# Token-ordered projection of the values, one-step transposes and another bank for statistics, in a one-core encoder layer

## The chip, the cores and the metric

The kernel runs on one core of a Trainium2 chip. The metric is the device time of one execution in microseconds (us). Below, TensorE is PE, VectorE is DVE, ScalarE is ACT, GpSimd is POOL and SyncE is SP in the profile; PEld is TensorE's loading of stationary operands.

## The reference

One layer of an encoder on x with 512 tokens of 2048 features, all float32. A normalised x is projected once, and two mixers read the projection:

```python
xn = rms_norm(x, attn_norm_g[l])
proj = jnp.einsum("bsd,dc->bsc", xn, w_in[l])            # 2048 -> 5 x 1024
u_val, u_gate, q, k, v = jnp.split(proj, split_pts, axis=-1)
y_conv = conformer_conv(u_val, u_gate, ...)   # gate, conv of 31 taps, LayerNorm over channels, silu
y_na = neighborhood_attention(heads(q), heads(k), heads(v), rpb[l])
mixed = concat([rms_norm(y_conv, ...), rms_norm(y_na, ...)])
x = x + mixed @ w_out[l]
# then: norm, up-projection to 2 x 5632, conv of 3 taps, silu(gate) * val, down-projection, residual, norm
```

The attention has 16 heads of 64. The tokens form a grid of 8 rows by 64 columns; a query at column c sees all 8 rows of 16 columns around c (clamped at the edges), with a learned bias by relative position.

## The kernel before, in words

**Data.** x lies with features on partitions: 16 tiles of 128 features x 512 tokens. The products are made to float32 accuracy out of three matmuls in a rounded format (mm3, L122): each operand is split into a high part and the rest, and high x high, high x low and low x high are summed in PSUM. Activations are split once (split, L155). Weights come in units of 128 x 1024 (512 KB, a DMA on SP, L109); ScalarE copies the high part (L114), VectorE subtracts for the low part (L115). weights() (L146) makes a unit three units (AHEAD) before it is used. A unit serves 8 slices of 128 features, so 24 matmuls of 128x512.

**Order of work.** The program is written as one stream of projection units. After each unit (or piece of one) tick (L132) advances two lists of generators, steps and asteps, by one yield each: what a generator does up to its next yield is put behind that unit's last matmul. A scheduler then lays out each engine's queue by priorities and these bounds; "pinned" instructions stay together, and shifted(600) lowers the priority of the convolution's taps. Each engine executes its queue in the order given.

**The input projection** follows ORDER (L51), "aaqaqaqaaqaqaqqq". An a is a pair of 128 gate channels and 128 value channels (glu, L321: two times 16 slices x 3 matmuls); gated (L326) multiplies by rstd, the reciprocal root of the tokens' mean square, takes the sigmoid, and runs the 31 taps on VectorE (L340, L343). A q is q, k and v of a pair of heads (qkv, L387), each 48 matmuls into one of three PSUM banks "mm"; VectorE evicts them, multiplied by rstd: q with tokens regrouped into four blocks of 16 columns (L395), k plainly (L399), v as four windows of 32 columns (L404).

**Attention of a pair** (attend, L409) is a generator: four loads of bias tables; eight transposes of v (L423) into two banks "tr", evicted by ScalarE as vt (L425); a yield; eight score matmuls (L437; each is two passes, so the profile counts 16) into a tile "sc" of two banks and the two "tr" banks, and the softmax of four 128x512 pieces: scale and bias (L444), maximum (L446) on VectorE, exp with sums on ScalarE (L449), reciprocal on VectorE (L450), normalisation on ScalarE (L452). After two or three yields turn(2) (L455) transposes the last two pieces (eight transposes, L462, evicted at L467 as pt); a yield later turn(0) the first two; two yields later the values (L476: 16 matmuls of 64 columns by 128, counted 32, into a bank "po") and their eviction ao (L496) with its sum of squares.

**Statistics.** rsqrt_steps (L170) sums over partitions with matmuls against ones (L182) into the bank tile "sc", computes the reciprocal root, and, after a yield, spreads it over partitions by two more matmuls (L201 to L217). group_a (L349) is the LayerNorm of the convolution's output: it sums the eight tiles on VectorE (L353, L355), takes the mean by a matmul (L358) into "sc", and goes on to ma, the split normalised tiles, and ra, the group's RMS factor. It is appended after pair NORM_AT = 5.

**Behind it:** norm_b (L534) normalises the attention's output into mb, yielding after every second tile. out_half (L523) projects ma, then mb, 16 tiles of 24 matmuls each, into the "mm" banks; read_a (L542) adds the first half to the residual as oa, from when ra is there. Then the gated MLP runs in chunks of four hidden tiles: up products (L672, L677), conv and activation, in_two (L773) splitting the hidden tile for the down products pd of the chunk, which follow in the next chunk. In the loop of chunks (L794) in_two of the first three tiles stands ahead of the fourth tile's up products, that of the fourth behind them.

PSUM has eight banks: "mm" three, "sc" a tile of two, "tr" two, "po" one. 512-token tiles in SBUF share one pool of 79.

Of the kernel before, what the change touches and what calls it, by code (L numbers as in the profile page):

```python
# [10 lines left out]
F32 = mybir.dt.float32  # L11
# [39 lines left out]
ORDER = "aaqaqaqaaqaqaqqq"  # L51
NORM_AT = 5
# [13 lines left out]
def layer(ctx: ExitStack, tc: tile.TileContext, xT, w_in, w_out, w_up, w_down, par, tab, out):  # L66
# [103 lines left out]
    def rsqrt_steps(accs, n, name, to=slice(0, S), keep=True):  # L170
# [22 lines left out]

        if not keep:
# [9 lines left out]
        yh = sm.tile([P, S // P], F32R, tag="rsh", name="rsh")  # L204
        nc.vector.tensor_copy(yh, y)
        nc.vector.tensor_sub(y, y, yh.bitcast(F32))
        ds = []
        for part in (yh.bitcast(F32), y):
# [4 lines left out]
        ps = psa.tile([P, 2, S], F32, tag="sc", name="st")[:, 0]  # L213
# [46 lines left out]
    for k in range(KD):  # L260
        x1.append(t2("x"))
        last = pin(nc.sync.dma_start(x1[k], xT[k]))
# [8 lines left out]
    a_, q_ = iter(range(NC_)), iter(range(NP_))  # L271
    for step in ORDER:
        i = next(a_ if step == "a" else q_)
        for n in ((NC_ + i, i) if step == "a" else (2 * NC_ + j * NP_ + i for j in range(3))):
            for u in range(KD // U):
                plan.append(lambda n=n, u=u: unit(w_in[n, :, u * U * P:(u + 1) * U * P], U * P))
# [4 lines left out]
    rstd, late = [], []  # L281

    def stats1():
# [6 lines left out]
        rstd.append((yield from rsqrt_steps(acc1, D, "rstd1")))  # L290
# [3 lines left out]
    def project(n):  # L294
# [9 lines left out]
        return ps  # L304

# [20 lines left out]
    def gated(i, pg, pv):  # L326
# [5 lines left out]
        nc.vector.tensor_mul(h, pv, g)  # L332
# [16 lines left out]
    def group_a():  # L349
# [7 lines left out]
        ps = psa.tile([P, 2, S], F32, tag="sc", name="st")[:, 0]  # L357
# [26 lines left out]
    def grid(t, c0, w):  # L384
        return t.rearrange("p (r c) -> p r c", c=GW)[:, :, c0:c0 + w]

    def qkv(p):  # L387
        got = []
        for j, nm in enumerate("qkv"):
            ps = project(2 * NC_ + j * NP_ + p)  # L390
            if nm == "q":

                t = t2(nm)
                by = "p (r b c) -> p r b c"
                nc.vector.tensor_mul(t.rearrange("p (b r c) -> p r b c", b=NB, r=WH),  # L395
                                     ps.rearrange(by, b=NB, r=WH), rstd[0].rearrange(by, b=NB, r=WH))
            elif nm == "k":
                t = t2(nm)
                nc.vector.tensor_mul(t, ps, rstd[0])  # L399
            else:  # L400

                t = [t2("vw").rearrange("p (b k) -> p b k", b=2) for _ in range(NB // 2)]
                for b in range(NB):
                    nc.vector.tensor_mul(t[b // 2][:, b % 2].rearrange("p (r c) -> p r c", c=KW), grid(ps, KC0[b], KW),  # L404
                                         grid(rstd[0], KC0[b], KW))
            got.append(t)
        return got

    def attend(p, q, k, v):  # L409


        hps = [slice(j * DH, (j + 1) * DH) for j in range(2)]
        tabs = {}
        for n in (2, 3, 0, 1):
            tabs[n] = t2("tab").rearrange("p (i k) -> p i k", i=2)
            i = nc.sync.dma_start(tabs[n], tab[2 * p + n % 2][:, n // 2:n // 2 + 2])
            if p == 0:
                pin(i)
        vt = []
        for half in range(2):  # L420
            ps = psa.tile([P, 4, P], F32, tag="tr", name="trv", bufs=2)
            for c in range(4):
                nc.tensor.transpose(ps[:, c, :], v[half][:, c // 2, c % 2 * P:(c % 2 + 1) * P], ident)  # L423
            t = t2("vt").rearrange("p (c k) -> p c k", c=4)
            nc.scalar.activation(t, ps, AF.Copy)  # L425
            vt.append(t)
        po = psa.tile([P, S], F32, tag="po", name="po")

        def scores():

            wide = psa.tile([P, 2, 2, 2 * P], F32, tag="sc", name="sc")
            banks = [wide[:, j] for j in range(2)]
            banks += [psa.tile([P, 2, 2 * P], F32, tag="tr", name="sc", bufs=2) for _ in range(2)]
            first = True
            for b in range(NB):
                for j, hp in enumerate(hps):
                    m = nc.tensor.matmul(banks[b // 2 * 2 + j][:, b % 2, :], q[hp, b * P:(b + 1) * P],  # L437
                                         grid(k, KC0[b], KW)[hp], start=True, stop=True)
# [508 lines left out]
```

## Time and profile before

| | |
|---|---|
| time, median of three runs | 2054.8 us (2051.95 to 2055.14) |
| the profiled execution | 2052.8 us, its span 2051.0 us |
| clock granted to TensorE | 0.998 of full speed |
| matmuls | 10816 |
| DMA traffic | 275.38 MB |

The profile is of one execution. Its page gives busy time by engine, forty slices of the span, DMA queues, the chain of work that ended last, and groups of instructions by line. Groups are read as line, engine, operation, output<-inputs, shapes, count | busy us, mean ns of one | idle time of the engine before them and who ended it. A row of the timeline gives the start and the length in us, the engine, the line, the operation and how many follow each other (x8); in brackets the idle time ahead of it and its releaser. Matmuls overlap, and their ends are modelled, so costs on TensorE are read from start to start.

### The profile page before, as it was taken

What the parts mean: (1) busy time and instruction counts of PE and PEld (TensorE: products, weight loads), DVE (VectorE), ACT (ScalarE), POOL (GpSimd) and SP (SyncE); (2) the same over time, 40 slices, a digit from 0 to 9 for tenths busy, and PEclk for the clock granted to TensorE, in tenths of its full rate; (3) what the DMA queues carried; (4) which work ended last, traced back from release to release, by engine and by line L of the source; (5) the groups of instructions that cost most, each with busy time, mean ns of one, the idle gap of its engine ahead of it and who ended that gap; (6) DMA issues with size and microseconds to landing.
All of it is one profiled execution on the core that took longest, in us unless ns stands there. A gap on an engine that the chain in (4) does not pass through costs nothing.

```text
span 2051.0 us, 28588 instructions
## 1 busy us (share of the span) xinstructions
PE 2031.7 (99%) x10816; PEld 1736.7 (85%) x10816; DVE 1666.7 (81%) x2319; ACT 1060.8 (52%) x1726; POOL 156.2 (8%) x186
## 2 busy tenths in 40 slices
PE   9999999999999999999999999999999999999997
PEld 7888888888788998888888888888888888888887
DVE  7996697686577898888878878888888888889876
ACT  6244424457436555555555555555554555555562
POOL 0000000000001001111111111111111111110110
PEclk9999999999999999999999999999999999999999
DMA  7332333236237435555555565565565565555682
GB/s 253 113 103 83 99 98 111 84 103 237 82 118 184 119 116 130 135 149 136 129 147 141 128 145 143 129 143 144 124 144 144 124 150 141 136 129 134 147 212 83
DMA packets 97209, 275.38 MB, mean 134 GB/s; under 512 B 10928, under 2 KB 11696, under 8 KB 97072
## 3 DMA queue, kind: packets, MB, share of 16 engines
q1 hardware_dynamic: 71712, 227.40, 35.0%
q0 software_dynamic: 25216, 46.15, 14.8%
q8 instruction: 85, 1.39, 0.3%
q14 instruction: 52, 0.43, 0.1%
q10 hardware_dynamic: 144, 0.01, 0.0%
HBM read 218.99 MB, written 54.53 MB: 133 GB/s over the span
## 4 chain that ended last, share of the span: by engine, by line
PE 97%; DVE 1%; DMA 0%; issue 0%; ACT 0%; DVEq 0%; ACTq 0%
PE pu L672 25%; PE pu L677 13%; PE pd L127 8%; PE pd L125 8%; PE pd L126 8%; PE pj L125 7%; PE pj L127 7%; PE pj L126 7%; PE po L125 3%; PE po L127 3%; PE po L126 3%; PE pu L125 1%; PE pu L127 1%; PE pu L126 1%; PE sc L437 1%; PE po L476 1%
## 5 line engine op out<-in xcount | busy, mean ns | idle before, releaser
L114 ACT ACTIVATE whi<-raw 128x1024 fp32r<-128x1024 f32 x364 | 384.4, 1058 | 486.8 <-PE pj L126 178.5
L115 DVE TENSOR_TENSOR wlo<-raw,whi 128x1024 fp32r<-128x1024 f32 x364 | 444.3, 1222 | 221.4 <-ACT whi L114 198.8
L672 PE MATMUL pu<-xc,whi 128*128 128x512 f32 x2240 | 574.7, 392 | 0.0
L672 PEld LDWEIGHTS pu<-xc,whi 128*128 128x128 f32 x2240 | 409.1, 189 | 74.0 <-ACT pl L684 0.2
L677 PEld LDWEIGHTS pu<-xc,wlo 128*128 128x128 f32 x2240 | 305.6, 190 | 21.9
L677 PE MATMUL pu<-xc,wlo 128*128 128x256 f32 x2240 | 312.3, 282 | 0.0
L125 PE MATMUL pd<-hh,whi 128*128 128x512 f32 x640 | 249.0, 391 | 2.6 <-ACT hh L775 2.6
L125 PE MATMUL pj<-xh,whi 128*128 128x512 f32 x640 | 251.1, 396 | 0.0
L127 PE MATMUL pj<-xh,wlo 128*128 128x512 f32 x640 | 249.7, 390 | 0.0
L126 PE MATMUL pj<-xl,whi 128*128 128x512 f32 x640 | 249.7, 390 | 0.0
L126 PE MATMUL pd<-hl,whi 128*128 128x512 f32 x640 | 249.2, 389 | 0.0
L127 PE MATMUL pd<-hh,wlo 128*128 128x512 f32 x640 | 249.2, 391 | 0.0
L791 POOL DMA_DIRECT2D x2d<-pdc x160 | 139.3, 872 | 1167.7 <-ACT pdc L790 949.5
L684 ACT ACTIVATE pl<-pu 128x256 f32<-128x256 f32 x280 | 104.5, 382 | 166.0 <-PE pu L672 165.9
L114 ACT ACTIVATE whi<-ws 128x1024 fp32r<-128x1024 f32 x132 | 139.8, 1059 | 78.1 <-PE pu L672 57.9
L343 DVE SCALAR_TENSOR_TENSOR y<-ch,prm,y 128x504 f32<-128x504 f32 (+14 forms) x240 | 173.7, 742 | 4.6
L115 DVE TENSOR_TENSOR wlo<-ws,whi 128x1024 fp32r<-128x1024 f32 x132 | 161.0, 1220 | 19.8 <-ACT whi L114 19.7
L127 PEld LDWEIGHTS pd<-hh,wlo 128*128 128x128 f32 x640 | 120.1, 188 | 28.8 <-DVE wlo L115 3.0
L125 PEld LDWEIGHTS pj<-xh,whi 128*128 128x128 f32 x640 | 120.2, 188 | 27.9 <-issue 3.7
L127 PEld LDWEIGHTS pj<-xh,wlo 128*128 128x128 f32 x640 | 120.2, 188 | 25.9 <-DVE wlo L242 0.4
L126 PEld LDWEIGHTS pj<-xl,whi 128*128 128x128 f32 x640 | 120.4, 188 | 25.0 <-DVE xl L265 0.7
L125 PEld LDWEIGHTS pd<-hh,whi 128*128 128x128 f32 x640 | 120.5, 188 | 24.9 <-ACT hh L775 3.0
(182 smaller groups left out, 2742.9 us busy)
## 6 DMA issues: line engine op xcount, KB each, us to landing
raw<-in_w_up SPq DMA_DIRECT2D x176, 512.0 KB, 3.6
raw<-in_w_down SPq DMA_DIRECT2D x88, 512.0 KB, 3.7
x2d<-pdc POOLq DMA_DIRECT2D x160, 256.0 KB, 4.7
raw<-in_w_in SPq DMA_DIRECT2D x76, 512.0 KB, 3.7
raw<-in_w_out SPq DMA_DIRECT2D x32, 512.0 KB, 3.9
x<-in_xT SPq DMA_DIRECT2D x32, 256.0 KB, 5.3
tab<-in_tab SPq DMA_DIRECT2D x32, 256.0 KB, 5.2
x2d<-x SPq DMA_DIRECT2D x16, 256.0 KB, 2.1
```

The lines of the kernel that those rows point to most:

```text
L114: i = nc.scalar.activation(hi[:, :n], raw[:, :n], AF.Copy)
L115: j = nc.vector.tensor_sub(lo[:, :n], raw[:, :n], hi[:, :n].bitcast(F32))
L125: nc.tensor.matmul(ps, hi[:, a], mh, start=start, stop=False)
L126: nc.tensor.matmul(ps, hi[:, a], ml, start=False, stop=False)
L127: return nc.tensor.matmul(ps, lo[:, a], mh, start=False, stop=stop)
L343: nc.vector.scalar_tensor_tensor(y[:, a:b], h[:, a + j - PAD:b + j - PAD], prm[:, o + j:o + j + 1], y[:, a:b], op0=ALU.mult, op1=ALU.add)
L437: m = nc.tensor.matmul(banks[b // 2 * 2 + j][:, b % 2, :], q[hp, b * P:(b + 1) * P], grid(k, KC0[b], KW)[hp], start=True, stop=True)
L476: m = nc.tensor.matmul(grid(po, b * BLK, BLK)[hp], vt[b // 2][:, 2 * (b % 2) + ch, hp], pts[b // 2 * 2 + j][:, 2 * (b % 2) + ch, :], start ...
L672: return nc.tensor.matmul(ps, w[0][:, k * P:(k + 1) * P], comb[c][k], start=k == 0, stop=k == U - 1)
L677: nc.tensor.matmul(ps[:, H:], w[1][:, k * P:(k + 1) * P], comb[c][k][:, :H], start=False, stop=False)
L684: nc.scalar.activation(to, ps, AF.Copy)
L791: nc.gpsimd.dma_start(xd[d], t, accum_op=ALU.add)
```

## The change

- **Order.** The values are no longer projected with each pair. ORDER becomes "aavaavaqaqaqaqqqqq": each v is a project_v of half of all value channels, after two gate/value pairs. The weights of the values come in units for two slices of features x 512 channels; x is now the stationary operand (128 tokens at a time) and the weights move, so that the result has tokens on partitions. Four banks are summed at once: the three "mm" and "po" for the first half, the two "tr" and "sc" for the second. ScalarE evicts them in ten pieces, scaled by the token's rstd: four tiles vg, and three tiles vx in which token groups are shifted by half a tile, for the windows of the middle blocks.
- **Token order.** For the projection tokens are ordered by groups of 8 columns (xG). The convolution's input, the attention's output and the tables are permuted where they are written or read; q is evicted plainly and k with a permutation. The transposes of v, vw and vt go.
- **Attention** becomes one generator over all pairs: tables; a yield; the values of the pair before directly ahead of this pair's scores, and the softmax in place in its tables, whose normalisation is one VectorE product with the reciprocal broadcast; three yields; all 16 transposes of the pair in one step, half of them into "sc"; a yield. The last pair's values come at the end.
- **Statistics** use the bank "po" instead of "sc" (with two sums, "po" then "sc"); the low part of the reciprocal root has a tile of its own. group_a is appended after pair 4.
- **norm_b** yields once, after the fifth tile. **In the first chunk** of the MLP in_two of all four tiles stands behind the fourth tile's up products.

The diff, cut to its core:

```diff
-ORDER = "aaqaqaqaaqaqaqqq"
-NORM_AT = 5
+ORDER = "aavaav" + "aq" * 4 + "qqqq"
+NORM_AT = 4
+NG = GW // 8
...
-        banks = [psa.tile([P, 2, S], F32, tag="sc", name="st")[:, 0]]
+        banks = [psa.tile([P, S], F32, tag="po", name="st")]
         if len(accs) > 1:
-            banks.append(psa.tile([P, S], F32, tag="po", name="st"))
+            banks.append(psa.tile([P, 2, S], F32, tag="sc", name="st")[:, 0])
...
+    vg, vx = [], []
+
+    def project_v(half):
+
+        if half:
+            sc = psa.tile([P, 2, S], F32, tag="sc", name="pv")
+            banks = [psa.tile([P, S], F32, tag="tr", name="pv", bufs=2) for _ in range(2)] + [sc[:, 0], sc[:, 1]]
+        else:
+            banks = [psm.tile([P, S], F32, tag="mm", name="pv") for _ in range(3)]
+            banks.append(psa.tile([P, S], F32, tag="po", name="pv"))
+        for u in range(KD // 2):
+            wh, wl = weights()[:2]
+            for k in range(2):
+                kk, f = 2 * u + k, slice(k * S, (k + 1) * S)
+                for t, ps in enumerate(banks):
+                    xh, xl = (x[:, t * P:(t + 1) * P] for x in xs[kk])
+                    nc.tensor.matmul(ps, xh, wh[:, f], start=kk == 0, stop=False)
+                    nc.tensor.matmul(ps, xl, wh[:, f], start=False, stop=False)
+                    m = nc.tensor.matmul(ps, xh, wl[:, f], start=False, stop=kk == KD - 1)
+            tick(m)
+            while late and rstd:
+                late.pop(0)()
+        y = rtok[0]
+        vg.append([t2("vg") for _ in banks])
+        vx.append([t2("vx") for _ in banks[1:]])
+        for t, ps in enumerate(banks):
+            nc.scalar.activation(vg[half][t], ps, AF.Copy, scale=y[:, t:t + 1])
+            for x, rows in ((t - 1, slice(0, DH)), (t, slice(DH, P))):
+                if 0 <= x < len(vx[half]):
+                    nc.scalar.activation(vx[half][x][rows], ps[rows], AF.Copy, scale=y[rows, t:t + 1])
...
-        nc.vector.tensor_mul(h, pv, g)
+        by = "p (g r c) -> p r g c"
+        nc.vector.tensor_mul(h.rearrange("p (r g c) -> p r g c", r=WH, g=NG), pv.rearrange(by, r=WH, g=NG),
+                             g.rearrange(by, r=WH, g=NG))
...
+    def values_of(p, b):
+        g, x = vg[p // 4], vx[p // 4]
+        return {0: (g[0], g[1]), 1: (x[0], x[1]), 2: (x[1], x[2]), 3: (g[2], g[3])}[b]
...
+    def softmax(banks, ts):
+        for n in (2, 3, 0, 1):
+            s = ts[n]
+            nc.vector.scalar_tensor_tensor(s, banks[n], DH ** -0.5, s, op0=ALU.mult, op1=ALU.add)
+            nm = sm.tile([P, 2], F32, tag="nm", name="nm")
+            nc.vector.tensor_reduce(nm, s, axis=AX.X, op=ALU.max, negate=True)
+            su = sm.tile([P, 2], F32, tag="su", name="su")
+            for i in range(2):
+                nc.scalar.activation(s[:, i], s[:, i], AF.Exp, bias=nm[:, i:i + 1], accum_out=su[:, i:i + 1])
+            nc.vector.reciprocal(su, su)
+            nc.vector.tensor_mul(s, s, su.unsqueeze(2).broadcast_to([P, 2, 2 * P]))
+
+    def turn(ts):
+        pts, first = {}, True
+        for n in (2, 3, 0, 1):
+            if n == 0:
+                wide = psa.tile([P, 2, 4, P], F32, tag="sc", name="trp")
+            ps = wide[:, n] if n < 2 else psa.tile([P, 4, P], F32, tag="tr", name="trp", bufs=2)
+            for i in range(2):
+                for ch in range(2):
+                    m = nc.tensor.transpose(ps[:, 2 * i + ch, :], ts[n][:, i, ch * P:(ch + 1) * P], ident)
                     if not first:
                         pin(m)
                     first = False
-            for n in (2, 3, 0, 1):
-                s = t2("s").rearrange("p (i k) -> p i k", i=2)
-                nc.vector.scalar_tensor_tensor(s, banks[n], DH ** -0.5, tabs[n], op0=ALU.mult, op1=ALU.add)
-                nm = sm.tile([P, 2], F32, tag="nm", name="nm")
-                nc.vector.tensor_reduce(nm, s, axis=AX.X, op=ALU.max, negate=True)
-                su = sm.tile([P, 2], F32, tag="su", name="su")
-                for i in range(2):
-                    nc.scalar.activation(s[:, i], s[:, i], AF.Exp, bias=nm[:, i:i + 1], accum_out=su[:, i:i + 1])
-                nc.vector.reciprocal(su, su)
-                for i in range(2):
-                    nc.scalar.activation(s[:, i], s[:, i], AF.Copy, scale=su[:, i:i + 1])
-                soft[n] = s
-
-        def turn(b0):
-            first = True
-            for j in range(2):
-                s = soft[b0 + j]
-                ps = psa.tile([P, 4, P], F32, tag="tr", name="trp", bufs=2)
-                for i in range(2):
-                    for ch in range(2):
-                        m = nc.tensor.transpose(ps[:, 2 * i + ch, :], s[:, i, ch * P:(ch + 1) * P], ident)
-                        if not first:
-                            pin(m)
-                        first = False
-                pt = t2("pt").rearrange("p (c k) -> p c k", c=4)
-                nc.scalar.activation(pt, ps, AF.Copy)
-                pts[b0 + j] = pt
-
-        def values():
-            first = True
-            for b in range(NB):
-                for ch in range(2):
-                    for j in (1, 0):
-                        hp = hps[j]
-                        m = nc.tensor.matmul(grid(po, b * BLK, BLK)[hp], vt[b // 2][:, 2 * (b % 2) + ch, hp],
-                                             pts[b // 2 * 2 + j][:, 2 * (b % 2) + ch, :], start=(ch == 0), stop=(ch == 1))
-                        if not first:
-                            pin(m)
-                        first = False
-
-        soft, pts = {}, {}
-        yield
-        scores()
-        yield
-        yield
-        if p < NORM_AT:
-            yield
-        turn(2)
-        yield
-        turn(0)
-        yield
-        yield
-        values()
+            pts[n] = t2("pt").rearrange("p (c k) -> p c k", c=4)
+            nc.scalar.activation(pts[n], ps, AF.Copy)
+        return pts
...
+    def attention():
+
+        before = None
+        for p in range(NP_):
+            while len(qk) <= p:
+                yield
+            ts = tables(p)
+            yield
+            if before:
+                values(*before)
+            banks = scores(p, not before)
+            softmax(banks, ts)
+            yield
+            yield
+            yield
+            pts = turn(ts)
+            yield
+            before = p, pts
+        yield
+        values(*before)
         yield
...
-            if i % 2:
+            if i == NP_ // 2:
...
-            if i == CH - 1:
+            if c and i == CH - 1:
                 hs = [in_two(h) for h in hs]
             hs.append(hidden(c * CH + i, lambda at: None if last else down(pend, down_units(c, i, at))))
-        hs[-1] = in_two(hs[-1])
+        hs = [h if isinstance(h, tuple) else in_two(h) for h in hs]
```

More of the change, by code (lines that the diff above doesn't have):

```diff
@@ L414, in attend, with tables @@
+    hps = [slice(j * DH, (j + 1) * DH) for j in range(2)]
+    def tables(p):
+        ts = {}
         for n in (2, 3, 0, 1):
-            tabs[n] = t2("tab").rearrange("p (i k) -> p i k", i=2)
-            i = nc.sync.dma_start(tabs[n], tab[2 * p + n % 2][:, n // 2:n // 2 + 2])
+            ts[n] = t2("tab").rearrange("p (i k) -> p i k", i=2)
+            i = nc.sync.dma_start(ts[n], tab[2 * p + n % 2][:, n // 2:n // 2 + 2])
             if p == 0:
                 pin(i)
[L419 to L433, printed above, removed]
-            first = True
[L435 to L438, printed above, removed]
+        return ts
@@ new lines, in scores @@
+    def scores(p, first):
+        q, k = qk[p]
+        wide = psa.tile([P, 2, 2, 2 * P], F32, tag="sc", name="sc")
+        banks = [wide[:, j] for j in range(2)]
+        banks += [psa.tile([P, 2, 2 * P], F32, tag="tr", name="sc", bufs=2) for _ in range(2)]
+        for b in range(NB):
+            for j, hp in enumerate(hps):
+                m = nc.tensor.matmul(banks[b // 2 * 2 + j][:, b % 2, :], q[hp, b * P:(b + 1) * P],
+                                     keys(k, b)[hp], start=True, stop=True)
+                if not first:
+                    pin(m)
+                first = False
+        return banks
@@ L510, in layer @@
             continue
+        if step == "v":
+            project_v(len(vg))
+            continue
         p += 1
-        steps.append(attend(p, *qkv(p)))
+        project_qk(p)
+        if p == 0:
+            steps.append(attention())
         if p == NORM_AT:
```

94 lines of the change are left out of this document (58 added, 36 removed).

## Prediction

> **What bounds the kernel now.** I read the page's busy times, its clock row and the engine shares of its chain first, then the waits of TensorE, then single stretches of the timeline.
>
> ```profile
> PE 2031.7 (99%) x10816; PEld 1736.7 (85%) x10816; DVE 1666.7 (81%) x2319; ACT 1060.8 (52%) x1726; POOL 156.2 (8%) x186
> ...
> PEclk9999999999999999999999999999999999999999
> ...
> PE 97%; DVE 1%; DMA 0%; issue 0%; ACT 0%; DVEq 0%; ACTq 0%
> ```
>
> TensorE is busy for 2031.7 of the span's 2051.0 us, at the full clock throughout, and the chain that ended last runs through it for 97%. All its idle time is 2051.0 - 2031.7 = 19.3 us, and much of that is the start and the end. So this kernel is a queue of matmuls without gaps: a microsecond is won where TensorE gets less to do or loses one of its few waits, and lost where another engine is late. Work moved between VectorE and ScalarE counts only through that. The two longest waits are these (line waited for, total, times, longest):
>
> ```profile
> PE pd L125 <- ACT hh L775: 2.6, 1, 2.6
> PE po L125 <- DVE oa L547: 1.9, 1, 1.9
> ```
>
> **The change part by part.** Positions in the new order are counted in its list of instructions. The projections keep their matmuls: the values took 8 pairs x 16 slices x 3 = 384 of 128x512, and now take 2 halves x 16 slices x 4 token tiles x 3 = 384 of the same shape, with x as the stationary operand instead of the weights. I count them at nothing: the same three kinds of operands (two high parts, one low) stream 512 columns behind a 128x128 load. What a group of other matmuls costs between projection matmuls, I take from start to start, since groups overlap their neighbours. The pitch first, then a group of values:
>
> ```profile
> 132.53 0.39 PE L127 MATMUL pj<-xh,wlo 128*128 128x512 f32 x1
> ...
> 133.21 0.39 PE L127 MATMUL pj<-xh,wlo 128*128 128x512 f32 x1
> 133.53 1.97 PE L476 MATMUL po<-pt,vt 128*64 128x128 f32 x32
> ...
> 135.76 0.40 PE L126 MATMUL pj<-xl,whi 128*128 128x512 f32 x1
> ```
>
> Three projection matmuls take 133.21 - 132.53 = 0.68 us, so one takes 0.227. From 133.21 to 135.76 stand two of them and the group: 2.55 - 0.45 = 2.10 us for the values of a pair.
>
> *A. The transposes of the values go.* One group of eight, and how many there are:
>
> ```profile
> 90.16 0.40 PE L127 MATMUL pj<-xh,wlo 128*128 128x512 f32 x1
> 90.39 1.03 PE L423 MATMUL trv<-ident,vw 128*128 128x128 f32 x8
> ...
> 91.50 0.39 PE L126 MATMUL pj<-xl,whi 128*128 128x512 f32 x1
> ```
>
> ```profile
> L423 PE MATMUL trv<-ident,vw 128*128 128x128 f32 x64 | 8.3, 272 | 0.0
> ```
>
> 91.50 - 90.16 = 1.34, less two pitches 0.45: 0.89 us for eight. There are 64, eight groups: **-7.1 us**. Nothing takes their place on TensorE, because the token-ordered projection delivers the values already turned. This is the firm term.
>
> *B and C. The small groups are entered less often.* One pair's scores stand whole; pair 6's were split in two:
>
> ```profile
> 96.52 0.39 PE L127 MATMUL pj<-xh,wlo 128*128 128x512 f32 x1
> 96.84 2.00 PE L437 MATMUL sc<-k,q 64*128 64x256 f32 x16
> ...
> 99.11 0.40 PE L126 MATMUL pj<-xl,whi 128*128 128x512 f32 x1
> ```
>
> ```profile
> 473.20 0.39 PE L127 MATMUL pj<-xh,wlo 128*128 128x512 f32 x1
> 473.52 1.14 PE L437 MATMUL sc<-k,q 64*128 64x256 f32 x8
> ...
> 474.92 0.40 PE L126 MATMUL pj<-xl,whi 128*128 128x512 f32 x1
> ```
>
> ```profile
> 484.69 0.39 PE L127 MATMUL pj<-xh,wlo 128*128 128x512 f32 x1
> 485.01 1.13 PE L437 MATMUL sc<-k,q 64*128 64x256 f32 x8
> ...
> 486.41 0.40 PE L126 MATMUL pj<-xl,whi 128*128 128x512 f32 x1
> ```
>
> Whole: 2.59 - 0.45 = 2.14. Each half: 1.72 - 0.45 = 1.27, together 2.54. Entering and leaving such a group once more costs 0.40 us. The new order keeps all scores whole: **-0.4** (B). In seven pairs the values of the pair before now stand directly ahead of the scores, so one entry and one exit go, but a border between two shapes (128x64 against 64x128) stays. I take half, 0.2 x 7 = **-1.4** (C); the ends are 0, if the border costs as much as both, and 7 x 0.40 = -2.8. The Trainium skill, "TensorEngine Tiling (Array Packing)", section Key Properties, says that changing the tiling mode drains TensorE; the trace agrees with its 0.40 us, and by that rule alone, with four changes per pair before and three after, C would lie at the same half. The 16 transposes of a pair's softmax come as 12 and 4, with a few projection matmuls between, where there were 8 and 8: the same number of groups, nothing (D; ends -0.4 x 8 and +0.4 x 8 if a group's length mattered, which the equal rows above don't suggest).
>
> *E. The wait of the output projection.* Its cause:
>
> ```profile
> 513.98 1.06 ACT L114 ACTIVATE whi<-raw 128x1024 fp32r<-128x1024 f32 x1 [6.50 <-PE po L126]
> ...
> 514.94 0.58 ACT L217 ACTIVATE ra<-st 128x512 f32<-128x512 f32 x1
> ...
> 516.21 1.28 DVE L547 TENSOR_TENSOR oa<-po,ra 128x512 f32<-128x512 f32 x2
> ...
> 516.95 0.50 PE L125 MATMUL po<-mah,whi 128*128 128x512 f32 x1 [1.90 <-DVE oa L547]
> ```
>
> The eviction of ra stood on ScalarE behind a weight copy that had itself waited 6.50 us for TensorE. In the new order ra comes 40 matmuls into the projection, and the bank is wanted some matmuls later: this wait goes, -1.9. But the fourth output tile needs the first one's bank, whose reading (oa) now stands on VectorE behind pair 6's softmax. It is wanted after the 16 score matmuls and 48 projection matmuls, 2.1 + 48 x 0.227 = 13.0 us after those scores start; the softmax needs 12.5 (below). I add 0.3 (0 to 3): **-1.6**.
>
> *F. The first down products.* All four in_two of chunk 0 now come at the chunk's end, and only nine matmuls of the first three tiles stand ahead of a 16-matmul up product; the fourth tile follows it.
>
> ```profile
> 776.86 1.22 DVE L115 TENSOR_TENSOR wlo<-ws,whi 128x1024 fp32r<-128x1024 f32 x1
> ...
> 778.72 0.63 ACT L775 ACTIVATE hh<-uy 128x512 fp32r<-128x512 f32 x1 [0.76 <-DVE uy L770]
> ```
>
> The old wait of 2.6 ends with the fourth hh (778.72). That one gets cover, but the first three are now made at the end too, behind the same VectorE work, to which the wlo at 776.86 belongs. So most of it stays: **-0.4** (-2.6 to +2).
>
> *H. A new wait: the mean of the convolution's group.* Where it stood before, in pair 5:
>
> ```profile
> 426.07 0.70 PE L437 MATMUL sc<-k,q 64*128 64x256 f32 x4
> ...
> 437.16 1.42 DVE L355 TENSOR_TENSOR acc<-acc,y 128x512 f32<-128x512 f32 x2
> ...
> 439.93 1.02 PE L358 MATMUL st<-acc,ones 128*128 128x512 f32 x2
> ```
>
> The sum over the eight tiles ended at 437.16 + 1.42 = 438.58, 12.5 us after the scores' start, and TensorE asked for it 1.3 us later. Now it is asked for after the 16 score matmuls and 49 projection matmuls, 2.1 + 49 x 0.227 = 13.2 us after the start, and VectorE has more to do by then: the normalisation of the softmax comes over from ScalarE. Its price is that of a whole 128x512 product on VectorE:
>
> ```profile
> L399 DVE TENSOR_TENSOR k<-pj,rstd 128x512 f32<-128x512 f32 x8 | 5.5, 684 | 0.0
> ```
>
> Four of 0.68 make 12.5 + 2.7 = 15.2 us, 2.0 to 2.2 too late. I take **+2.2** (0, if the adds go ahead of the normalisations, to 5, with two weight subtractions of 1.22 more in front). Behind the waiting matmul all of TensorE's queue stands.
>
> *G and I. The rest.* The first half of the values takes banks that still hold a gate/value pair. An eviction of rstd, then twice three products of 0.68 and a sigmoid, each eviction as long as this one,
>
> ```profile
> L425 ACT ACTIVATE vt<-trv 128x512 f32<-128x512 f32 x16 | 8.5, 584 | 0.0
> ```
>
> is 0.58 + 2 x 2.63 = 5.8 us; 22 projection matmuls and 17 of the first banks cover 8.9. **+0.3** (0 to 2). The ten evictions after each half take 10 x 0.58 = 5.8 us of ScalarE; the three units of weights ahead (24 matmuls, 5.4 us each) cover them, and they would cost up to 5.8 without that cover. The start of the second output half: the norm of the attention yields once instead of four times, so that 72 + 48 matmuls of work lie otherwise; 0 (0 to 2). VectorE's and ScalarE's own balance lies beside TensorE.
>
> Sum: -7.1 - 0.4 - 1.4 - 1.6 - 0.4 + 0.3 + 2.2 + 0 = **-8.4 us**. The profiled execution took 2052.8 us (span 2051.0), so 2044.4 for it. It lies 2.0 below the median of 2054.8; against the median, **2046.4**.
>
> **The rivals.** *1, a larger gain.* H's adds come in time, C is at its full 2.8, and E and F vanish: -7.1 - 0.4 - 2.8 - 1.9 - 2.6 = -14.8, 2040. For it: the margins missed are of 2 us. Against: it asks for four things at once.
>
> *2, the gain is given back in queues.* Two engines work strictly in order; the ra row above (6.50 us behind a copy) shows what that does. With H at 5, E's new wait at 3, F at 0: -7.1 - 0.4 - 1.4 + 1.1 + 0 + 0.3 + 5 = -2.5, 2052.3, no change that a measurement can tell. For it: five joints are rearranged together with VectorE nearly full where attention and convolution meet. Against: each joint is met once, not once per pair. The Trainium skill, "TensorE: Matmul & The Clock Gate", opening table, says that ScalarE and VectorE have strict first-in-first-out queues and only TensorE pulls weight loads ahead; it speaks against the change, whose evictions wait for TensorE ahead of weight copies, and by it the outcome would be this rival's. The trace agrees in the ra row alone.
>
> *3, slower: the softmax chain becomes the bound in every pair.* All 16 transposes now wait for it at once:
>
> ```profile
> 158.33 0.92 PE L437 MATMUL sc<-k,q 64*128 64x256 f32 x6
> ...
> 170.04 0.90 ACT L452 ACTIVATE s<-s,su 128x256 f32<-128x256 f32 x2
> ...
> 176.76 1.03 PE L462 MATMUL trp<-ident,s 128*128 128x128 f32 x8
> ```
>
> The last normalisation ended at 170.94, 12.6 us after the scores' start, and the first transposes began at 18.4. The new order asks for the first twelve at 2.1 + 72 x 0.227 = 18.4 us, with 12.6 + 2.7 = 15.3 to be had: 3 us spare. VectorE in the early stage:
>
> ```profile
> 90.00:150.00 60.00, 60.00 (x307) 49.35 (x306) 57.27 (x84) 25.09 (x45) 0.00 (x0) 1.00 0.33 101
> ```
>
> It was busy for 57.27 of 60 us, so that a convolution's taps (31 per tile) could slip between the softmax's steps. The rival decides from 18.4 us on: at 21, each of eight pairs waits 2.6, +20.8, and the kernel takes 2067. Against: the taps have lowered priority, and the chain measured here held in that full stage.
>
> **How the numbers follow.** About 0.2%, 4.1 us, is what a measurement of this kernel can tell from no change: under 2050.7 is faster, over 2058.9 slower. The forecast (2042 to 2050.7) has 0.60, rival 1 (2038 to 2042) 0.13, rival 2 (2050.7 to 2058.9) 0.15, rival 3 and several upper ends together (above) 0.12. Faster: 0.73, same 0.15, slower 0.12. The range 2040 to 2056 leaves out half of rival 1, a small part of rival 2, and rival 3: 0.2.
>
> **What would show it.** Right: no transposes of values in the groups; values directly ahead of scores with 0.2 us less than the two groups here; TensorE's waits led by the group's mean on acc (about 2) and a first down product; the value projection at 0.227 us a matmul; transposes 18.4 us after the scores without a wait. Wrong: a wait of transposes on the normalisation in several pairs (rival 3), a pitch above 0.227 in the values' projection (nothing above allows for one: at 0.237 it would cost 384 x 0.010 = 3.8), waits on weight copies behind the evictions, or an mm bank late for the value projection.

## The result, and the profile after

The changed kernel takes 2045.76 us (median of 6 executions, 2044.16 to 2047.44), the kernel before 2054.61 (6, 2051.95 to 2055.97): ratio 0.9959, 95% interval 0.9946 to 0.9971. The gain is 8.85 us; the forecast was 8.4, 2046.4.

The busy times and the clock of the page of the changed kernel's first profile (2047.1 us, span 2045.3):

```profile
PE 2025.5 (99%) x10752; PEld 1731.9 (85%) x10752; DVE 1672.8 (82%) x2319; ACT 1035.4 (51%) x1662; POOL 156.2 (8%) x186
...
PEclk9999999999999999999999999999999999999998
```

10816 - 10752 = 64: the transposes of the values are gone. TensorE is still busy for 99% of the span. Its waits in that profile (line waited for, total, times, longest):

```profile
PE rb L204 <- DVE dg L200: 1.9, 1, 1.9
PE idle L254 <- DVE warm L251: 1.6, 1, 1.6
PE st L399 <- DVE acc L396: 1.3, 1, 1.3
PE st L218 <- DVE dg L213: 1.1, 1, 1.1
PE st L183 <- DVE acc L169: 0.9, 1, 0.9
PE trp L499 <- DVE tab L489: 0.9, 1, 0.9
...
PE pu L126 <- ACT rstd L220: 0.7, 1, 0.7
```

The two longest waits of before, for oa (1.9) and for hh (2.6), are both gone. New are the mean of the convolution's group (st L399), one transpose (trp L499), and two that nobody had listed: st L218 and pu L126, which both belong to the statistics between output projection and MLP.

This execution ran at a mean granted clock of 0.996, the profiled one of before at 0.998, and the two spans differ by 5.7 us only. A second profile of the same changed kernel, with 0.998, took 2043.6 us (span 2041.8): at equal clocks the gain is 2052.8 - 2043.6 = 9.2. It belongs to a second measurement of five executions, one of which took 4103.5 us in a slow state and is left out of every comparison, so that 2045.42 is the median of the other four. The two profiles of the changed kernel differ at one place above all. First the windows (length, PE, PEld, DVE, ACT, POOL busy, granted clock, DMA share, GB/s) of the one with 2047.1, then those of the one with 2043.6:

```profile
690.00:695.00 5.00, 3.13 (x19) 2.33 (x18) 4.86 (x12) 1.93 (x3) 0.00 (x0) 0.96 0.50 168
695.00:700.00 5.00, 5.00 (x33) 5.00 (x33) 3.21 (x6) 0.61 (x1) 0.00 (x0) 0.70 0.00 0
```

```profile
690.00:695.00 5.00, 3.14 (x20) 2.34 (x19) 4.86 (x11) 1.93 (x3) 0.00 (x0) 1.00 0.31 115
695.00:700.00 5.00, 5.00 (x44) 5.00 (x43) 4.73 (x8) 1.88 (x2) 0.00 (x0) 1.00 0.00 0
```

TensorE pauses for 1.9 of the first 5 us in both. In the first profile the granted clock falls to 0.70 behind it, and 33 matmuls go through where 44 do in the second. The pause is part of the kernel; its aftermath comes in some executions.

### The profile page after: what moved, and what is told of

The parts are those of the page before. It is cut to its first block, busy times and chain, and to the rows that moved or that the text cites. A ratio compares the mean times of both kernels' runs of the same rounds, so it can differ in the third digit from the quotient of the medians.

```text
span 2045.3 us, 28399 instructions
## 1 busy us (share of the span) xinstructions
PE 2025.5 (99%) x10752; PEld 1731.9 (85%) x10752; DVE 1672.8 (82%) x2319; ACT 1035.4 (51%) x1662; POOL 156.2 (8%) x186
## 4 chain that ended last, share of the span: by engine, by line
PE 95%; DVE 2%; ACT 1%; DMA 1%; issue 1%; SPq 0%; DVEq 0%; ACTq 0%
PE pu L723 25%; PE pu L728 13%; PE pd L128 8%; PE pd L126 8%; PE pd L127 8%; PE pj L128 5%; PE pj L127 5%; PE pj L126 5%; PE po L126 3%; PE po L127 3%; PE po L128 3%; PE pv L330 1%; PE pv L332 1%; PE pv L331 1%; PE pu L126 1%; PE pu L128 1%
## 5 line engine op out<-in xcount | busy, mean ns | idle before, releaser
L126 PE MATMUL pd<-hh,whi 128*128 128x512 f32 x640 | 248.9, 391 | 0.0
L127 PE MATMUL pj<-xl,whi 128*128 128x512 f32 x512 | 200.4, 391 | 0.1
L128 PE MATMUL pj<-xh,wlo 128*128 128x512 f32 x512 | 200.0, 391 | 0.0
L126 PE MATMUL pj<-xh,whi 128*128 128x512 f32 x512 | 198.6, 392 | 0.4 <-ACT xh L267 0.4
L384 DVE SCALAR_TENSOR_TENSOR y<-ch,prm,y 128x500 f32<-128x500 f32 (+14 forms) x240 | 173.4, 741 | 4.5
L127 PEld LDWEIGHTS pd<-hl,whi 128*128 128x128 f32 x640 | 120.3, 188 | 25.0
L126 PEld LDWEIGHTS pd<-hh,whi 128*128 128x128 f32 x640 | 120.5, 188 | 21.9
L841 ACT ACTIVATE pdc<-pd 128x512 f32<-128x512 f32 x160 | 93.8, 588 | 84.1 <-PE pd L128 84.1
L126 PEld LDWEIGHTS pj<-xh,whi 128*128 128x128 f32 x512 | 96.0, 188 | 22.3 <-issue 1.7
```

The source lines that it names most:

```text
L126: nc.tensor.matmul(ps, hi[:, a], mh, start=start, stop=False)
L127: nc.tensor.matmul(ps, hi[:, a], ml, start=False, stop=False)
L128: return nc.tensor.matmul(ps, lo[:, a], mh, start=False, stop=stop)
L384: nc.vector.scalar_tensor_tensor(y[:, a:b], h[:, a + j - PAD:b + j - PAD], prm[:, o + j:o + j + 1], y[:, a:b], op0=ALU.mult, op1=ALU.add)
```

## The experiments

All times are medians, beside runs of the kernel before on the same chip; "changed" is the changed kernel.

**The anchor.**

> The changed kernel once more, as the anchor for the runs beside it: 0.4% below the kernel before, about 2046 us. Two theories of where its 9 us come from. Theory T (terms on TensorE): the transposes of the values give 7.1, the values set next to the scores 1.5, the two old waits 4.5, and about 5 are given back at single places (the group's mean 1.3, a pair's transposes 0.9, and above all the statistics between output projection and MLP, where the trace shows waits of 1.1 and 0.7 us and then a stretch at a lower granted clock). Rival R: the gain is that of fewer waits alone, and the transposes were covered.

Measured 2045.42 (2043.60 to 2046.29) against 2054.31 (0.9956, 0.9943 to 0.9970).

**The transposes of the values put back.** In attention, behind the tables:

```diff
             ts = tables(p)
+            for half in range(2):
+                ps = psa.tile([P, 4, P], F32, tag="tr", name="trv", bufs=2)
+                for c in range(4):
+                    nc.tensor.transpose(ps[:, c, :], vg[p // 4][2 * half + c // 2][:, c % 2 * P:(c % 2 + 1) * P], ident)
+                nc.scalar.activation(t2("vt").rearrange("p (c k) -> p c k", c=4), ps, AF.Copy)
             yield
```

> Eight transposes per pair of value tiles that are there already, with their two evictions, put back where the tables are loaded; nobody reads them. Theory T: 8 x 0.89 = 7.1 us slower than the changed kernel, no new wait. Rival R: well under 3 us, since they would be covered.

2052.90 against 2054.31 (0.9994, 0.9985 to 1.0003): 7.5 us above the changed kernel measured beside it (2045.42), 7.1 above the changed kernel's first median (2045.76). In the profiles the stretch from the first projection matmul to the first up product is 675.5 us long, against 668.4 in the changed kernel's second: 7.1. One group of its timeline:

```profile
231.65 0.40 PE L128 MATMUL pj<-xh,wlo 128*128 128x512 f32 x1
231.89 1.04 PE L535 MATMUL trv<-ident,vg 128*128 128x128 f32 x8
...
232.99 0.39 PE L127 MATMUL pj<-xl,whi 128*128 128x512 f32 x1
```

232.99 - 231.65 = 1.34, less two pitches 0.45: 0.89, as before. Term A is shown to be the gain's main part, and rival R falls.

**The statistics' bank.** In the MLP the seventh of the up products uses the bank "po", as the statistics now do. The edit lets the statistics of the MLP's norm alone use "sc":

```diff
-        banks = [psa.tile([P, S], F32, tag="po", name="st")]
+        bank = lambda: (psa.tile([P, 2, S], F32, tag="sc", name="st")[:, 0] if apart else
+                        psa.tile([P, S], F32, tag="po", name="st"))
+        banks = [bank()]
...
-        ps = psa.tile([P, S], F32, tag="po", name="st")
+        ps = bank()
...
-        rstd2.append((yield from rsqrt_steps(acc2, D, "rstd2")))
+        rstd2.append((yield from rsqrt_steps(acc2, D, "rstd2", apart=True)))
```

> Only the statistics of the MLP's norm go back from the bank of the seventh up product into the two-bank tile. Theory T: the spreading matmuls stand 41 up matmuls behind the sums instead of 28, so the waits of 1.1 and 0.7 us go, and with them the stretch at a granted clock of 0.7 (some 1.5 us): 3 to 4 us faster than the changed kernel. Rival: the clock falls there for another reason (the wait on xc ahead of it is in both kernels), and then only 1.8 come back; or the place is hidden, and nothing does.

> The changed kernel with the MLP's statistics in the two-bank tile, once more, as the anchor for the three beside it (its times lay closest together): about 2043.6 us.

Measured 2043.61 (2042.87 to 2043.72; 0.9948, 0.9935 to 0.9960) and, beside other runs, 2043.37 (2042.18 to 2043.67; 0.9942, 0.9929 to 0.9954). The first is 1.8 us below the changed kernel beside it (2045.42). That is less than the 3 to 4 expected and just the rival's figure, so the medians do not tell the two apart. The traces do: the stretch from the first up product to the 61st matmul of the down products takes 132.2 us in the changed kernel's first profile, 130.0 in its second, and 128.7 and 128.5 in the two here. By that the pause costs 1.3 to 1.5 us, and the first profile loses another 2.2, about 1.7 of it to the fall of the clock (3.41 us at a granted clock of 0.50, as the last section shows) and 0.4 to a wait of the sums on acc. All ten executions here were recorded at a mean clock of 0.997 and lie within 1.5 us; of the changed kernel's ten six were recorded at 0.996, and they lie within 3.8. The same windows of the first of the two:

```profile
690.00:695.00 5.00, 4.99 (x40) 4.71 (x39) 4.86 (x12) 2.96 (x4) 0.00 (x0) 1.00 0.33 120
695.00:700.00 5.00, 5.00 (x44) 5.00 (x43) 5.00 (x9) 1.09 (x2) 0.00 (x0) 1.00 0.19 61
```

No pause, no fall. How the pause arises, in the timeline of the changed kernel's first profile:

```profile
691.06 0.28 PE L128 MATMUL pu<-xc,wlo 128*128 128x256 f32 x1
692.47 1.01 PE L218 MATMUL st<-dg,ones 128*128 128x512 f32 x2 [1.14 <-DVE dg L213]
694.17 0.39 PE L126 MATMUL pu<-xc,whi 128*128 128x256 f32 x1 [0.69 <-ACT rstd L220]
```

The up product that needs "po" must stay behind the statistics, so the spreading matmuls stand 28 up matmuls behind the sums instead of 41, before their operand dg is there; the next product then waits until ScalarE has read the bank. This is the fastest kernel of the study, faster than both.

**The pause filled.** On the changed kernel, with the statistics left in "po":

```diff
+        idle = psa.tile([P, 2, S], F32, tag="sc", name="fill") if name == "rstd2" else None
+        for i in range(5 if name == "rstd2" else 0):
+            m = nc.tensor.matmul(idle[:, 0, :1], ones, y[:, 0:1], start=True, stop=True)
...
         for i, dg in enumerate(ds):
             nc.tensor.matmul(ps, ones_r, dg, start=i == 0, stop=i == 1)
+        for i in range(3 if name == "rstd2" else 0):
+            pin(nc.tensor.matmul(idle[:, 1], ones_r, comb[0][i], start=True, stop=True))
```

> The changed kernel, its MLP statistics still in the result's bank, but the two waits there (1.1 and 0.7 us) are filled with matmuls that nobody reads: five of one column on the finished reciprocal root ahead of the spreading matmuls, three of 512 columns behind them. They do not shorten the wait. If TensorE's pause is what lowers the granted clock behind it in some executions (0.70 in 695 to 700 us of the first profile), the clock stays at 1.00 there and the median comes 1 to 2 us below the changed kernel's 2045.9, with a narrower spread. Rival: the clock falls at that time of its own accord, and the median stays at 2046 or rises by what the filling costs.

2044.27 (2044.04 to 2046.68; 0.9955, 0.9942 to 0.9967), 1.5 and 1.2 us below the changed kernel's two medians, with the clock at 1.00 in the profile. The size fits, but the spread is not narrower, and one of the changed kernel's profiles has 1.00 there as well. More is to be had from all runs together: these five executions were recorded at 0.997 as well, and among the traces of changed kernels the fall at this place stands in three of the four with the pause (the first profile, the transposes put back and the normalisation on ScalarE) and in none without it. So the pause is its cause; why it does not always follow is shown in the last section. Why two executions here took 2045.6 and 2046.7 stays open.

**The normalisation on ScalarE again.**

```diff
-            nc.vector.tensor_mul(s, s, su.unsqueeze(2).broadcast_to([P, 2, 2 * P]))
+            for i in range(2):
+                nc.scalar.activation(s[:, i], s[:, i], AF.Copy, scale=su[:, i:i + 1])
```

> The softmax is normalised on ScalarE again, 64 operations in place of 32 on VectorE. If the normalisation on VectorE makes the sum of the convolution's group late, as the prediction had it, the wait for the mean (1.3 us) and the transposes' wait of pair 5 (0.9) go: 1 to 2 us faster than the changed kernel. Rival: the mean waits because of the interleaving with the softmax, or the scheduler asks for it earlier in turn: within 1 us of the changed kernel.

2045.94 (0.9959, 0.9946 to 0.9971), 0.5 above the changed kernel beside it. Its timeline around the mean:

```profile
429.07 0.69 DVE L396 TENSOR_TENSOR acc<-acc,y 128x512 f32<-128x512 f32 x1
...
429.91 1.10 PE L399 MATMUL st<-acc,ones 128*128 128x512 f32 x2 [1.24 <-DVE su L488]
```

With 34 projection matmuls between scores and mean instead of 49, the scheduler asks for the sum 3.4 us earlier, as it is ready earlier, and TensorE waits 1.2 again (the profile names the reciprocal su, which ended 0.1 us after the sum). The rival holds: where the mean stands is no fixed deadline. The transposes' wait of 0.9 did go, but waits of 0.5 and 0.3 on the two parts of weights came.

**The first chunk's in_two as before.**

```diff
-            if c and i == CH - 1:
+            if i == CH - 1:
```

> On top of the anchor, the first chunk's in_two of three tiles goes back ahead of the fourth tile's up products. If the wait of 2.6 us on the fourth hh, which is in the trace of the kernel before and not in that of the changed one, comes from that order, it returns: 2.5 to 3 us slower than the anchor. Rival (the prediction's step F): the first down products wait for the same VectorE work either way, 0.4 us or less.

2044.94, 1.6 above its anchor (0.9951, 0.9939 to 0.9964), and its first wait is the old one:

```profile
PE pd L126 <- ACT hh L828: 2.0, 1, 2.0
```

The same part alone, on the kernel before:

> The kernel before with one part of the change alone: in the first chunk in_two of all four tiles stands behind the fourth tile's up products. If the wait of 2.6 us on the fourth hh comes from that order alone, this is 2 to 2.6 us faster than the kernel before, about 2052.3. Rival (the prediction's F): 0.4 us, nothing to be seen.

2052.82 against 2054.76 (0.9992, 0.9983 to 1.0001), 1.9 faster; the wait on hh is gone from its list, that on oa is not:

```profile
PE po L125 <- DVE oa L547: 1.9, 1, 1.9
PE rb L201 <- DVE dg L197: 1.9, 1, 1.9
```

Both ways the edit is worth about 2 us, not 0.4; each single comparison is near the measurement's limit, the waits are not.

**Values and scores apart.**

```diff
             ts = tables(p)
-            yield
             if before:
                 values(*before)
+            yield
```

> On top of the anchor, the values of the pair before come one unit ahead of the scores, with 24 projection matmuls between. Theory: one border between shapes against an exit and an entry is worth 0.22 us, seven times 1.5, so 1.5 us slower, less what the other places of pair 5's transposes and of the mean give or take (1 us). Rival: the adjacency is worth nothing, 0.

2046.23 against 2054.92 (0.9957, 0.9944 to 0.9971): 2.9 above the anchor, but its profiled execution took 2043.93, 1.8 above the anchor's. What the border is worth is read better from the timelines. The changed kernel, then this one:

```profile
284.99 0.39 PE L128 MATMUL pj<-xh,wlo 128*128 128x512 f32 x1
285.31 0.66 PE L514 MATMUL po<-pt,vg 128*64 128x128 f32 x8
...
287.21 2.00 PE L472 MATMUL sc<-k,q 64*128 64x256 f32 x16
...
289.47 0.39 PE L127 MATMUL pj<-xl,whi 128*128 128x512 f32 x1
```

```profile
279.35 0.39 PE L128 MATMUL pj<-xh,wlo 128*128 128x512 f32 x1
279.67 0.66 PE L516 MATMUL po<-pt,vg 128*64 128x128 f32 x8
...
281.90 0.40 PE L127 MATMUL pj<-xl,whi 128*128 128x512 f32 x1
```

Together 4.48 - 0.45 = 4.03; the values alone 2.55 - 0.45 = 2.10, and the scores 2.14 as before. 4.24 - 4.03 = 0.21 a pair, 1.5 in seven. In the profiles, too, the stretch from the first projection matmul to the first up product is 1.4 longer than the anchor's (669.0 against 667.6). The rest of the 2.9 isn't explained; the four executions that weren't profiled took 2.2 to 2.8 us more than the profiled one and were recorded at 0.996 instead of 0.997, which fits a fall of the clock, but none of them has a trace.

**The transposes one unit earlier.**

```diff
             yield
             yield
-            yield
             pts = turn(ts)
```

> On top of the anchor, the transposes of a pair come after two yields instead of three: 48 projection matmuls, 13.0 us behind the scores' start instead of 18.4. In the changed kernel's trace the softmax ends 11.7 to 14.6 us after the scores' start (25 in pair 5). If that chain sets the limit, TensorE now waits up to 1.5 us in the pairs 1 to 4 and more in pair 5: 3 to 10 us slower, with waits of trp on the normalisation. Rival: the last quarter's five matmuls later are cover enough and the shorter order saves as much: within 2 us of the anchor.

2044.76 (0.9950, 0.9937 to 0.9962), 1.4 above the anchor: the rival's case. From 230 to 420 us, where the pairs 0 to 3 are, TensorE waits for nothing at all; the waits on transposes are these, later:

```profile
PE trp L501 <- DVE su L490: 0.6, 1, 0.6
...
PE trp L501 <- DVE tab L491: 0.2, 1, 0.2
```

So even 13.0 us behind the scores the softmax is not the bound, and the slower rival of the prediction was further off than it said. The softmax moved with the demand: its last normalisation ends 11.4 to 12.0 us after the scores' start in these pairs, in the changed kernel 11.7 to 14.6.

**The mean later.** On the kernel with the statistics apart, one yield more ahead of the mean, then two:

```diff
             nc.vector.tensor_add(acc, acc, ys[i])
         yield
+        yield
         ps = psa.tile([P, S], F32, tag="po", name="st")
```

> The statistics of the MLP in the two-bank tile, and one yield more ahead of the group's mean. Its matmul moves only three projection matmuls back (0.7 us of the 1.3), but the order around pair 5 changes: its transposes come as twelve and four again instead of four single groups. Theory: the wait of 0.9 us there goes and 0.6 of the mean's: 1.5 us below the anchor's 2043.4, about 2042. Rival: the waits move on to the statistics behind, no difference.

> The same with two yields more: the mean is asked for 84 matmuls behind the scores, its wait of 1.3 us goes wholly; 2041 to 2042 if nothing takes its place. Rival: the group's later steps, now crowding at the start of the output projection, bring a wait on ra or on the split tiles: above 2043.

2053.45 (0.9997, 0.9988 to 1.0006) and 2050.59 (0.9983, 0.9974 to 0.9992): 10 and 7 us slower than without, the clearest misses here. The first wait of the one with one yield, ScalarE's timeline ahead of it, and the windows behind it:

```profile
PE po L126 <- ACT whi L115: 5.4, 1, 5.4
```

```profile
480.70 0.61 ACT L165 ACTIVATE acc<-y 128x512 f32<-128x512 f32 x1
481.22 3.73 ACT L168 ACTIVATE sq<-y 128x512 f32<-128x512 f32 x7
484.86 1.99 ACT L115 ACTIVATE whi<-raw 128x1024 fp32r<-128x1024 f32 x2
```

```profile
486.00:488.00 2.00, 1.97 (x5) 1.61 (x6) 2.00 (x4) 2.00 (x4) 0.00 (x0) 0.50 1.01 379
488.00:490.00 2.00, 2.00 (x8) 1.59 (x7) 2.00 (x3) 0.46 (x2) 0.00 (x0) 0.50 1.02 418
```

The LayerNorm's work on ScalarE, pushed later, stands ahead of the copies of weights for the output projection; TensorE waits 5.4 us and then runs at half the clock for another 5.7, to 491.77. The Trainium skill, "TensorE: Matmul & The Clock Gate", opening table, says that ScalarE's queue is strictly in order; the trace agrees, with seven squares (3.73 us) ahead of the copy that TensorE waits for. The second kernel's waits are others (3.2 us on dg, 2.0 on ao, 1.4 on oa), and its clock stands at 0.50 from 503.86 to 514.10.

## Why the prediction was right, and where it was not

Measured terms are from the second profile, which has the clock of the profile before, unless another is named.

| step | predicted | measured | from |
|---|---|---|---|
| A, value transposes | -7.1 | -7.1 | groups of 0.89; 7.1 to 7.5 when put back |
| B, scores whole | -0.4 | -0.4 | no split scores |
| C, values beside scores | -1.4 | -1.5 | seven times 0.21 |
| D, transposes as 12 and 4 | 0 | +0.7 | 0.13 in five pairs, 0.08 in one |
| E, ra | -1.6 | -1.9 | wait gone, none new |
| F, first down products | -0.4 | -2.6 | wait gone; 1.6 and 1.9 in the experiments |
| G, value banks and evictions | +0.3 | 0 | no such wait |
| H, mean | +2.2 | +1.3 | the wait |
| I, second output half | 0 | 0 | no such wait |
| not foreseen: pair 5's transposes | | +0.9 | the wait |
| not foreseen: MLP statistics | | +1.8 | waits of 1.1 and 0.7 |
| sum | -8.4 | -8.8 | -9.2 at equal clocks |

The total was right, and its core was: A to C were priced from start to start and came out within 0.1 us each, and the values' projection keeps its pitch (its 192 matmuls a half start 0.227 us apart). The closeness is in part luck: F gave 2.2 us more than forecast, and two costs that were nowhere in the sum took 2.7.

**D.** The step reckoned a group's price as independent of its length and counted groups. Two groups of eight cost 1.78; in the changed kernel's timeline twelve and four cost more:

```profile
255.87 0.40 PE L128 MATMUL pj<-xh,wlo 128*128 128x512 f32 x1
256.10 1.47 PE L499 MATMUL trp<-ident,tab 128*128 128x128 f32 x12
...
257.65 0.39 PE L127 MATMUL pj<-xl,whi 128*128 128x512 f32 x1
...
258.34 0.40 PE L127 MATMUL pj<-xl,whi 128*128 128x512 f32 x1
258.64 0.66 PE L499 MATMUL trp<-ident,tab 128*128 128x128 f32 x4
...
259.37 0.39 PE L126 MATMUL pj<-xh,whi 128*128 128x512 f32 x1
```

1.78 - 0.45 = 1.33 for twelve, 1.03 - 0.45 = 0.58 for four, 1.91 in all.

**F failed.** "The first three are now made at the end too, behind the same VectorE work", said the step, and kept most of the wait. It did not stay. With in_two behind, the last tile's product came ahead of weight subtractions on VectorE. In the kernel before, the subtraction at 776.86 stood ahead of that product (777.99) and hh came 4.3 us after the first down product began (774.38); in the kernel with the statistics apart the product (766.04) follows the first down product (765.31) by 0.7 us, ahead of the subtraction at 767.24. The kernel before with this part alone has the same new order (776.42 ahead of 777.62), and putting the part back restored the old one. The row of 776.86 was quoted, but as something fixed, when its place is the scheduler's choice.

**H, the right mechanism, too large.** The scores of pair 4 start at 419.09 in the second profile; the sum and the mean there:

```profile
432.19 1.41 DVE L396 TENSOR_TENSOR acc<-acc,y 128x512 f32<-128x512 f32 x2
...
433.74 1.10 PE L399 MATMUL st<-acc,ones 128*128 128x512 f32 x2 [1.32 <-DVE acc L396]
```

The sum ends 433.60 - 419.09 = 14.5 us after the scores start (15.2 predicted), and is asked for at 432.4, 13.3 after (13.2). That the normalisation on VectorE makes the sum late is borne out by its experiment; that the kernel would be faster without it is not.

**Left out: the statistics' other places.** The prediction followed the new bank through attention and output projection (E), and did not ask who else uses "po". It is the seventh up product. Its waits are 1.8 us, and in some executions the fall of the clock comes on top. The softmax rival had its price right per pair but its threshold too near: the chain ends 11.4 to 14.6 us after the scores start in all pairs but the sixth (25 us, where the split tiles of ma stand between), and even asked for at 13.0 us the first twelve transposes didn't wait.

**Where the terms lie.** Between the two profiles at equal clocks the stretch from the first projection matmul to the first up product shrank by 7.9 us (676.3 to 668.4), where A to E, G to I and pair 5's transposes give 8.0, and the stretch behind it, to the end of the last matmul, by 0.8, where F and the MLP statistics give 0.8. The remaining 0.5 of the 9.2 lies ahead of the first projection matmul, which starts at 5.56 us instead of 6.05. That is no effect of the change as far as is known: two profiles of one kernel, the one with the statistics apart, have 5.69 and 5.99.

## What to carry to other kernels

In a kernel whose TensorE never rests, price a removed group of matmuls from the start of the matmul ahead of it to the start of one behind it; here each such forecast held to a tenth of a microsecond. When a buffer changes its role, list every later user of the new place, not only those near the edit. Moving a piece of work one step away from its wait can be far dearer than the wait: here 1.3 us of waiting were traded for 10.

## What the runs showed of the hardware

A short pause of TensorE costs more than itself, though not always. In the traces' records of the granted clock a fall is a stretch at 0.50 that lasts 3.41 us or a whole number of these: once behind the pauses of 1.1 and 0.7 us in the changed kernel's first profile (694.57 to 697.99), twice around the end of the wait of 5.4 us (484.94 to 491.77), three times in the kernel with the mean two yields later. Six traces have such a stretch between start and end, and in each of them its borders lie a whole number of steps of 3.413 us ahead of the last change of the clock, at the end of the program. Counted in these steps, the first profile has the whole pause in one step, and the second (no fall, last change at 2032.40) has a border within it:

```profile
691.16:694.57 3.41, 1.54 (x7) 0.77 (x6) 3.34 (x7) 1.93 (x3) 0.00 (x0) 1.00 0.39 141
694.57:697.98 3.41, 3.41 (x18) 3.41 (x18) 3.10 (x6) 0.00 (x0) 0.00 (x0) 0.50 0.00 0
```

```profile
687.55:690.96 3.41, 2.88 (x25) 2.67 (x23) 2.92 (x9) 1.63 (x3) 0.00 (x0) 1.00 0.73 211
690.96:694.37 3.41, 2.08 (x11) 1.49 (x12) 3.41 (x6) 1.38 (x3) 0.00 (x0) 1.00 0.26 101
```

In the first TensorE is without a matmul for 3.41 - 1.54 = 1.87 us of one step, and the next step runs at 0.50; in the second for 0.53 and 1.33, and nothing falls. In all traces, ahead of the end, a step at full clock with up to 1.44 us without a matmul was followed by no fall at all, one with 1.57 (the transposes put back) and each with 1.87 or more by one, and one with 1.66 by none. That last one is the kernel before, behind its wait on oa; with in_two moved alone the same wait of 1.9 lies within one step, and the clock falls. So where a pause lies in these steps, which differs between two profiles of one kernel, goes far to decide whether the clock falls behind it, and a fall of one step costs about 1.7 us more. The exact limit stays open: at the end of the program, where some matmuls have a single column, 0.94 us were enough. The Trainium skill, "TensorE: Matmul & The Clock Gate", section "What's actually happening", lets the clock fall after an idle window of about 3.4 us whose phase runs freely; the length and the free phase agree with these traces, but here a window was enough in which TensorE paused for about half the time.

The mean granted clock of an execution also sorts the kernel before: of its 51 executions beside these experiments, those recorded with 0.998 took 2051.8 to 2053.2 us, those with 0.996 2053.8 to 2057.0, so profiles are best compared at equal clocks.
